# One pass for both blocks of local attention, paired cross scores, one first transfer and another landing time

## The chip, the cores and the metric

The kernel runs on one core of a Trainium2 chip. The metric is the device time of one execution in microseconds. The core's engines run side by side, each with its own queue in order: TensorE (PE) multiplies matrices, VectorE (DVE) and ScalarE (ACT) work on elements, GpSimd (POOL) and SyncE (SP) issue transfers (DMA) from and to memory. An engine that needs another's result waits on a semaphore.

## The reference

One step of a decoder layer for a prompt of 256 tokens and 8 sequences of 8 new tokens each (320 columns together), width 2048, in fp32. Cut to what matters:

```python
z = rmsnorm(x, g_mix) @ w_in            # B, C, h, local q/k/v, cross q
y_conv = b * short_conv(c * h)
y_swa  = sink_attention(q, k, v, bias, valid, sink)   # 8 heads, 2 kv heads, window 128
mk, mv = memory_kv(mem_prompt)          # 256 memory tokens
y_x    = cross_attention(qx, mk, mv)    # 4 heads
x = x + concat(y_conv, y_swa, y_x) @ w_out
x = x + square(relu(rmsnorm(x, g_mlp) @ w_up)) @ w_down
```

Local attention of the prompt goes by blocks of 128 queries. A block sees itself and the block before, with a band mask of 128 positions and a relative-position bias; each head has a learned sink in the softmax's denominator. So the first block has 128 keys and the second 256, of which any query sees at most 128: key j of the block before is seen by a query i only if i < j, and key j of the own block only if i >= j. A new token of a sequence sees 128 cached keys and those of its own 8 tokens. Cross attention of the sequences reads 256 cached memory tokens each.

## The kernel before

All activations lie with channels in the partitions and the 320 tokens in the free dimension. fp32 accuracy comes from splitting: a weight or activation is divided into a high part (ACT rounds it) and a low part (DVE subtracts), and PE multiplies high by high, high by low, low by high: three main matmuls for a product. Weights come in pieces of 512 KB (128 partitions, 2 x 512 columns) into `raw`; `split_piece` makes `wh` and `wl`. Four pieces may be loaded and four split ahead of PE.

The program is written out by one Python pass. The main work is a list of units, each 12 main matmuls of the projections (6 wider ones for the memory's weights): cross queries, local keys and values, memory keys and values, local queries, C, h, B, then output, up and down projections. Between units, `boundary` lets side jobs take a step: the norm of x (`rb_job`, `mean_rsqrt`), the heads' norms (`start_head`), the memory (`mem_job`), cross attention of prompt and sequences (`cross_prompt`, `cross_sample`), local attention (`swa_prompt`, `swa_sample`), the convolution. What a job issues in a step stands between two units in every engine's queue: on PE a burst of small matmuls, named "ax" by the PSUM tile that they write; the main ones are "mm".

Where a job steps is set by `Pace`, a running estimate of each engine's clock made while the program is written. A job that needs a tile yields in `after` until the estimate says that the tile was ready 0.2 us ago on PE's clock. A load counts as landed LAG us after its estimated transfer (2 us for weights). These estimates only set the order; at run time semaphores keep it right, and a burst that was set too early makes PE wait.

What the prediction's steps touch: `rb_job` squares the four blocks of x (tiles `lx`) on ACT and adds them up on DVE. `mean_rsqrt` then takes the mean over the partitions with `mean_over`: ACT makes the high part of the sum, DVE the low part, PE multiplies both by a matrix of 1/2048 (`mean_d`). From this comes rb, with which every projection's result is scaled. `start_head` does the same for each head, with `mean_h`. At the start, `cols` (all gain columns, 252 bytes for each partition) and the first 320 columns of x come by ACT's queue; 10 matmuls on a tile of ones run on PE ahead of the first main one. `cross_sample` computes four sequences at a time: scores of one sequence are four matmuls, one for each head, in 32-column tiles of the array; its values are eight. `swa_prompt` does two heads, one block after the other. `swa_sample` does four sequences for one kv head. The tiles that side jobs use are `w2` (12 of 512 columns), `z` (10 of 336) and four PSUM banks.

The profile names nearly every instruction by line 166, the helper in `Paced` through which all of them are issued.

Of the kernel before, what the change touches and what calls it, by code (L numbers as in the profile page):

```python
# [34 lines left out]
LAG = 6.0  # L35
WARM = 10
# [9 lines left out]
def arrange(inputs):  # L46
# [15 lines left out]
    out["cols"] = np.concatenate([a[n].reshape(-1, P) for n, _ in ROWS]).T  # L62
# [5 lines left out]
def constants():  # L68
# [11 lines left out]
    for r in row:  # L80
# [4 lines left out]
        "c_ident": np.eye(P, dtype=np.float32),  # L85
        "c_hot": hot,
# [161 lines left out]
def trunk_step(ctx: ExitStack, tc: tile.TileContext, I, O):  # L248
# [29 lines left out]

    def zt(cols=336):
        return zs.need([P, 336])  # L280
# [14 lines left out]
    act.dma_start(out=cols[:, 0:63], in_=I["cols"])  # L295
# [9 lines left out]
    dve.memset(ones_h, 1.0 / 128)  # L305
    ones_d = const.tile([P, P], F32, name="ones_d")
    dve.memset(ones_d, 1.0 / D)
    mean_h = const.tile([P, P], F32R, name="mean_h")
    dve.tensor_copy(out=mean_h, in_=ones_h)
    mean_d = const.tile([P, P], F32R, name="mean_d")  # L310
    dve.tensor_copy(out=mean_d, in_=ones_d)
# [12 lines left out]
    def gcol(name, i=0):  # L324
        return cols[:, col[name] + i:col[name] + i + 1]
# [82 lines left out]
    def split_piece():  # L408
# [9 lines left out]
        if i < 2:  # L418

            for c in range(2):  # L420
                k = 2 * i + c
                x = xblk[0][:, k, :]
                if k:
                    split_act(S0h[:, k, :], S0l[:, k, :], x, gcol("g_mix", k))
                else:
                    dve.tensor_scalar(out=S0h[:, k, :], in0=x, scalar1=gcol("g_mix", k), scalar2=None, op0=ALU.mult)
                    dve.scalar_tensor_tensor(out=S0l[:, k, :], in0=x, scalar=gcol("g_mix", k),
                                             in1=S0h[:, k, :].bitcast(F32), op0=ALU.mult, op1=ALU.subtract)
# [149 lines left out]
    def rb_job():  # L578
        for b in range(4):
            act.activation(out=xblk[b], in_=xblk[b], func=AF.Square)  # L580
# [155 lines left out]
    def mk_evac(t, ps):  # L736
        z = w2.must([P, 512])
# [118 lines left out]
    def cross_sample(f):  # L856
# [15 lines left out]
        for _ in range(2):  # L872
            yield from load()
        sb = yield from bank()
        for b in range(4):
            cur = queue.pop(0)
            yield from after(*cur)
# [5 lines left out]
            yield from load()  # L883
# [50 lines left out]
    def sink_softmax(s, nh, sinks, nsinks):  # L934
        nm, es, den = sm()[:, 0:nh], sm()[:, 0:nh], sm()[:, 0:nh]
        dve.tensor_reduce(out=nm, in_=s, axis=AX.X, op=ALU.max, negate=True)
        dve.tensor_tensor(out=nm, in0=nm, in1=nsinks, op=ALU.min)
        dve.tensor_tensor(out=es, in0=sinks, in1=nm, op=ALU.add)
        yield from after(es)
        for i in range(nh):  # L940
# [5 lines left out]
        for i in range(nh):  # L946
            dve.tensor_scalar(out=s[:, i, :], in0=s[:, i, :], scalar1=den[:, i:i + 1], scalar2=None, op0=ALU.mult)

    def swa_prompt(g, hp):
# [7 lines left out]
        for blk in range(2):  # L957
            nkb = 1 + blk
            nk = nkb * P
            q0 = blk * P  # L960
            bk = yield from bank()
            for i in range(2):
                pe.matmul(out=bk[:, i * nk:(i + 1) * nk], lhsT=qT[:, hs + i, q0:q0 + P], rhs=kT[:, g, 0:nk],
                          start=True, stop=True)
            yield 1
            s = yield from half()
            s3 = s[:, 0:2 * nk].rearrange("p (h k) -> p h k", h=2)
            dve.scalar_tensor_tensor(out=s3, in0=bk[:, 0:2 * nk].rearrange("p (h k) -> p h k", h=2), scalar=SC,
                                     in1=b3[:, :, 256 - nk:256], op0=ALU.mult, op1=ALU.add)
            ax.put(bk)  # L970
            yield from sink_softmax(s3, 2, skb[:, hs:hs + 2], nskb[:, hs:hs + 2])
            yield from after(s)
            bk = yield from bank()
            for kb in range(nkb):
                for i in range(2):
                    c = (kb * 2 + i) * P
                    pe.transpose(bk[:, c:c + P], s3[:, i, kb * P:(kb + 1) * P], ident)
            yield 1
            pt = yield from half()
            act.activation(out=pt[:, 0:2 * nk], in_=bk[:, 0:2 * nk], func=AF.Copy)  # L980
            ax.put(bk)
# [420 lines left out]
```

## Time and profile before

| | us |
|---|---|
| median of 3 runs | 1315.78 |
| lowest, highest | 1315.7, 1315.86 |
| the profiled execution's own time | 1315.88 |
| its span, first to last instruction | 1313.8 |
| busy: PE, DVE, ACT, POOL | 1309.0, 675.2, 540.3, 18.4 |
| mean granted TensorE clock | 1.0 |

The span is counted from the first instruction; 2.1 us lie around it. In the profile a group reads "out<-in": the tile written and the tiles read, buffer numbers left out. A row of the timeline gives start, duration, engine, line and operation, and in brackets the idle time ahead of it with what ended it. A PE matmul's record covers its pipeline too, so records overlap and what counts is the distance from start to start. An fp32 matmul stands there as two records, a transpose or an fp32r matmul as one.

### The profile page before, as it was taken

Reading aid. Unit: us, or ns where it says so; the run is one execution under the profiler, and the core shown is the slowest. Engines: PE = TensorE matmul, PEld = TensorE weight load, DVE = VectorE, ACT = ScalarE, POOL = GpSimd, SP = SyncE. Lnnn points to the kernel's source line nnn. Section 1 sums busy time; section 2 is a strip of 40 time slices with the busy share of each in tenths; the row PEclk is TensorE's granted clock in tenths of the full one; section 3 lists DMA queues with packets and bytes.
Section 4 is the critical chain, followed back from the end, with each engine's and each line's share of the span. In section 5 each row is a group of like instructions: output and inputs, shape, how many; then the busy total and the mean of one; then the engine's idle time right before and its main releaser. Section 6 shows DMA issues by size and latency. Waiting matters only on the chain.

```text
span 1313.8 us, 21565 instructions
## 1 busy us (share of the span) xinstructions
PE 1309.0 (100%) x8956; PEld 1287.4 (98%) x8956; DVE 675.2 (51%) x1025; ACT 540.3 (41%) x801; POOL 18.4 (1%) x37
## 2 busy tenths in 40 slices
PE   9999999999999999999999999999999999999998
PEld 9988999999999999999999999999999999999998
DVE  7876665776576445443345443345443344444342
ACT  7683554343355444322344422334432324433321
POOL 1011000000000000000000000000000000000000
PEclk9999999999999999999999999999999999999999
DMA  8767555356344443444443444443444444444552
GB/s 298 254 208 273 180 173 198 132 190 249 129 159 148 156 147 128 161 158 149 156 148 129 161 158 149 154 150 128 161 159 148 155 149 129 160 157 150 176 167 73
DMA packets 65488, 217.03 MB, mean 165 GB/s; under 512 B 8437, under 2 KB 10717, under 8 KB 65360
## 3 DMA queue, kind: packets, MB, share of 16 engines
q1 hardware_dynamic: 63184, 210.14, 47.9%
q0 software_dynamic: 1776, 5.26, 1.2%
q8 instruction: 70, 1.15, 0.4%
q10 hardware_dynamic: 432, 0.28, 0.1%
q14 instruction: 26, 0.21, 0.0%
HBM read 211.53 MB, written 7.65 MB: 167 GB/s over the span
## 4 chain that ended last, share of the span: by engine, by line
PE 96%; DMA 1%; ACT 1%; DVE 1%; issue 1%; ACTq 0%; DVEq 0%; SPq 0%
PE mm L166 92%; PE ax L166 3%; DMA raw<-in_w_in 1%; DMA lx<-in_xT 1%; ACT wh L166 0%; DVE wl L166 0%; DVE lx L166 0%; ACT lx L166 0%; DVE S1l L166 0%; DVE S0l L166 0%; ACT w L166 0%; ACT S1h L166 0%; ACT S0h L166 0%; DVE z L166 0%; ACTq L166 0%
## 5 line engine op out<-in xcount | busy, mean ns | idle before, releaser
L166 DVE TENSOR_TENSOR wl<-raw,wh 128x1024 fp32r<-128x1024 f32 (+1 forms) x362 | 436.1, 1217 | 476.5 <-ACT wh L166 475.4
L166 ACT ACTIVATE wh<-raw 128x1024 fp32r<-128x1024 f32 (+1 forms) x362 | 374.4, 1050 | 631.6 <-PE mm L166 595.6
L166 PE MATMUL mm<-S0h,wh 128*128 128x320 f32 x1472 | 456.2, 311 | 0.0
L166 PE MATMUL mm<-S0h,wl 128*128 128x320 f32 x1472 | 453.0, 309 | 0.0
L166 PE MATMUL mm<-S0l,wh 128*128 128x320 f32 x1472 | 452.8, 309 | 0.0
L166 PE MATMUL mm<-S1h,wh 128*128 128x320 f32 x1280 | 397.3, 310 | 0.4 <-DVE lx L166 0.4
L166 PE MATMUL mm<-S1h,wl 128*128 128x320 f32 x1280 | 395.5, 309 | 0.0
L166 PE MATMUL mm<-S1l,wh 128*128 128x320 f32 x1280 | 395.5, 309 | 0.0
L166 PEld LDWEIGHTS mm<-S0h,wh 128*128 128x128 f32 x1472 | 276.3, 188 | 2.8 <-issue 2.7
L166 PEld LDWEIGHTS mm<-S0l,wh 128*128 128x128 f32 x1472 | 276.0, 188 | 0.1
L166 PEld LDWEIGHTS mm<-S0h,wl 128*128 128x128 f32 x1472 | 275.9, 188 | 0.1
L166 PEld LDWEIGHTS mm<-S1h,wh 128*128 128x128 f32 x1280 | 240.3, 188 | 1.1 <-ACT wh L166 0.6
L166 PEld LDWEIGHTS mm<-S1l,wh 128*128 128x128 f32 x1280 | 240.4, 188 | 0.1
L166 PEld LDWEIGHTS mm<-S1h,wl 128*128 128x128 f32 x1280 | 240.3, 188 | 0.0
L166 DVE TENSOR_TENSOR lx<-mm,lx 128x320 f32<-128x320 f32 (+1 forms) x97 | 46.9, 486 | 80.6 <-PE mm L166 75.3
L166 ACT ACTIVATE z<-z 128x320 f32<-128x320 f32 (+1 forms) x118 | 55.1, 470 | 65.3 <-DVE z L166 64.2
L166 DVE TENSOR_TENSOR S1l<-z,S1h 128x320 fp32r<-128x320 f32 x68 | 33.3, 490 | 51.1 <-ACT S1h L166 51.1
L166 ACT ACTIVATE S1h<-z 128x320 fp32r<-128x320 f32 x68 | 32.1, 472 | 9.0 <-DVE z L166 6.9
L166 DVE SCALAR_TENSOR_TENSOR z<-mm,r2b 128x320 f32<-128x320 f32 x64 | 31.0, 484 | 0.0
L166 PE MATMUL mm<-wh,S1h 128*128 128x512 f32 x64 | 25.7, 401 | 0.0
L166 PE MATMUL mm<-wh,S1l 128*128 128x512 f32 x64 | 25.1, 392 | 0.0
L166 PE MATMUL mm<-wl,S1h 128*128 128x512 f32 x64 | 25.0, 390 | 0.0
(162 smaller groups left out, 433.1 us busy)
## 6 DMA issues: line engine op xcount, KB each, us to landing
raw<-in_w_up SPq DMA_DIRECT2D x128, 512.0 KB, 3.3
raw<-in_w_down SPq DMA_DIRECT2D x128, 512.0 KB, 3.3
raw<-in_w_in SPq DMA_DIRECT2D x54, 512.0 KB, 4.0
raw<-in_w_out SPq DMA_DIRECT2D x32, 512.0 KB, 3.5
raw<-in_w_mem_k SPq DMA_DIRECT2D x8, 512.0 KB, 4.7
raw<-in_w_mem_v SPq DMA_DIRECT2D x8, 512.0 KB, 3.9
w<-in_cmk SPq DMA_DIRECT2D x16, 256.0 KB, 5.2
w<-in_cmv SPq DMA_DIRECT2D x16, 256.0 KB, 4.6
```

Of the source, the lines that this page charges most:

```text
L166: return f(*args, **kw)
```

## The change

It has six parts.

1. **Local attention of the prompt in one pass.** Both blocks of two heads are scored together into two PSUM banks (`banks`). For the second block the scores against the block before (`prev`) and against its own keys are laid over each other with a maximum: at each place just one of the two is not masked. So a row of the softmax has 128 places for either block, and one softmax serves four rows of heads. The transposed weights are divided again by a triangle of ones (`tri`, a new constant that POOL loads): `low` is the part for the own block, and the rest belongs to the block before. The value product is one matmul over all four for the first block's values and one more, over 256 columns, for the second's.
2. **Local attention of the sequences**: `swa_sample` now does all eight for a kv head in one job.
3. **Cross scores**: `cross_sample` waits for two sequences' keys and issues their matmuls in one step; the loads follow by twos.
4. **The start**: the gain columns and the first block of x come in one transfer, into a `w2` tile named `first`; DVE copies the columns out. The first four channel blocks take their gain straight from `first`. In `rb_job` the first block's square is two instructions, since its parts lie in two tiles. The table load on ACT now stands ahead of the transfer. WARM is 8 for 10, and one tile serves for both mean matrices.
5. **The clock**: LAG is 5.5 for 6.0. With it, and with the other jobs, every decision of `Pace` may fall elsewhere.
6. `mk_evac` runs the side jobs until the memory job is done, if it isn't.

```diff
-LAG = 6.0
-WARM = 10
+LAG = 5.5
+WARM = 8
...
+    def banks():
+
+        while sum(last is None or pace.idle(last) for _, last in ax.free) < 2:
+            yield 1
+        return ax.must([P, 512]), ax.must([P, 512])
...
-    act.dma_start(out=cols[:, 0:63], in_=I["cols"])
...
     def rb_job():
         for b in range(4):
-            act.activation(out=xblk[b], in_=xblk[b], func=AF.Square)
+            if b:
+                act.activation(out=xblk[b], in_=xblk[b], func=AF.Square)
+            else:
+                act.activation(out=xblk[0][:, 0, :], in_=first[:, 63:63 + T], func=AF.Square)
+                act.activation(out=xblk[0][:, 1:4, :], in_=xblk[0][:, 1:4, :], func=AF.Square)
+                w2.put(first)
...
     def mk_evac(t, ps):
+        side.until(["mem"])
...
         for _ in range(2):
             yield from load()
+        yield from after(*queue[0], *queue[1])
         sb = yield from bank()
         for b in range(4):
             cur = queue.pop(0)
-            yield from after(*cur)
+            yield from after(*cur, *(queue[0] if b % 2 == 0 else ()))
...
             w2.put(*cur)
-            yield from load()
+            if b % 2:
+                yield from load()
+                yield from load()
...
+        bk, fk = yield from banks()
+        for i in range(2):
+            pe.matmul(out=bk[:, i * 256:(i + 1) * 256], lhsT=qT[:, hs + i, P:TP], rhs=kT[:, g, 0:TP],
+                      start=True, stop=True)
+            pe.matmul(out=fk[:, i * P:(i + 1) * P], lhsT=qT[:, hs + i, 0:P], rhs=kT[:, g, 0:P], start=True, stop=True)
...
+        dve.tensor_tensor(out=s[:, 256:512], in0=s[:, 256:512], in1=prev[:, 0:256], op=ALU.max)
...
+        for r in range(4):
+            pe.transpose(bk[:, r * P:(r + 1) * P], s4[:, r, :], ident)
+        yield 1
+        pt = yield from half()
+        low = yield from zt()
+        dve.tensor_tensor(out=pair(low[:, 0:256]), in0=pair(bk[:, 256:512]),
+                          in1=tri.rearrange("p (o k) -> p o k", o=1).to_broadcast([P, 2, P]), op=ALU.mult)
+        act.activation(out=pt, in_=bk, func=AF.Copy)
+        dve.tensor_tensor(out=pt[:, 256:512], in0=pt[:, 256:512], in1=low[:, 0:256], op=ALU.subtract)
...
+        pe.matmul(out=bk, lhsT=vnat[:, 0, g * P:(g + 1) * P], rhs=pt, start=True, stop=False, skip_group_check=True)
+        pe.matmul(out=bk[:, 256:512], lhsT=vnat[:, 1, g * P:(g + 1) * P], rhs=low[:, 0:256], start=False, stop=True,
+                  skip_group_check=True)
...
+    def swa_sample(g):
...
+        pool.dma_start(out=tri, in_=I["c_tri"])
...
-    load_x(0, 0, 1, act)
+
+    first = w2.must([P, 512])
+    act.dma_start(out=first[:, 0:63 + T], in_=I["cols"])
```

How the instructions stand, before and after, at the three places that the prediction speaks of. Numbers in the names count the tiles made.

PE where the mean over x is taken: the pair on `mean_d` between main matmuls of the local key and value group. mm_524 is that group's first output tile in both programs; the second is mm_548 before and mm_546 now, the third mm_565 before. Before:

```order
L166 MATMUL mm_548<-S0h_116,wh_420 128x320
L166 MATMUL mm_548<-S0l_117,wh_420 128x320
L166 MATMUL mm_548<-S0h_116,wl_421 128x320
L166 MATMUL ax_3_498<-z_2_499,mean_d_104 128x320
L166 MATMUL ax_3_498<-z_3_500,mean_d_104 128x320
L166 MATMUL mm_565<-S0h_116,wh_388 128x320
```

Now:

```order
L167 MATMUL mm_524<-S0h_115,wh_421 128x320
L167 MATMUL mm_524<-S0l_116,wh_421 128x320
L167 MATMUL mm_524<-S0h_115,wl_422 128x320
L167 MATMUL ax_3_497<-z_2_498,mean_d_99 128x320
L167 MATMUL ax_3_497<-z_3_499,mean_d_99 128x320
L167 MATMUL mm_546<-S0h_115,wh_389 128x320
```

The pair stands behind the first tile's 12 matmuls instead of the second's: main matmuls 0 to 203 are ahead of it instead of 0 to 215. The first burst on `mean_h` moves likewise, from 348 main matmuls to 324, and holds two heads instead of one.

DVE ahead of that pair: the additions of squares (lx), the low parts of the memory's blocks (S1l), four small ones on the sinks, and the low part of the sum (z_3). Before:

```order
L166 TENSOR_TENSOR wl_421<-raw_275,wh_420 128x1024
L166 SCALAR_TENSOR_TENSOR S1l_119<-w2_1_315,cols_92,S1h_118 128x256
L166 TENSOR_TENSOR lx_1_127<-lx_1_127,lx_3_145 128x1280
L166 TENSOR_TENSOR lx_1_127<-lx_1_127 128x640
L166 TENSOR_TENSOR lx_1_127<-lx_1_127 128x320
L166 SCALAR_TENSOR_TENSOR S1l_119<-w2_1_315,cols_92,S1h_118 128x256
L166 TENSOR_TENSOR sm_468<-skb_109,sel_110 128x8
L166 TENSOR_REDUCE skc_111<-sm_468 128x2
L166 TENSOR_SCALAR nskc_113<-skc_111 128x2
L166 TENSOR_SCALAR nskb_112<-skb_109 128x8
L166 SCALAR_TENSOR_TENSOR S1l_119<-w2_2_317,cols_92,S1h_118 128x256 x2
L166 TENSOR_TENSOR z_3_500<-lx_1_127,z_2_499 128x320
```

Now:

```order
L167 TENSOR_TENSOR wl_422<-raw_274,wh_421 128x1024
L167 TENSOR_TENSOR lx_1_131<-lx_1_131,lx_3_145 128x1280
L167 TENSOR_TENSOR lx_1_131<-lx_1_131 128x640
L167 TENSOR_TENSOR lx_1_131<-lx_1_131 128x320
L167 SCALAR_TENSOR_TENSOR S1l_118<-w2_2_314,cols_92,S1h_117 128x256
L167 TENSOR_TENSOR sm_467<-skb_108,sel_109 128x8
L167 TENSOR_REDUCE skc_110<-sm_467 128x2
L167 TENSOR_SCALAR nskc_112<-skc_110 128x2
L167 TENSOR_SCALAR nskb_111<-skb_108 128x8
L167 SCALAR_TENSOR_TENSOR S1l_118<-w2_2_314,cols_92,S1h_117 128x256
L167 SCALAR_TENSOR_TENSOR S1l_118<-w2_3_316,cols_92,S1h_117 128x256
L167 TENSOR_TENSOR z_3_499<-lx_1_131,z_2_498 128x320
```

One S1l ahead of the additions is gone, and a memory block's two halves now lie one behind the additions and one behind the small ones. On ACT the square of that block (it waits for the second half), one S1h and then the high part z_2 follow each other, without the two copies and the S1h that stood between before. Further on in DVE's queue, rb and the first heads' scaling by it stand one weight split sooner than before.

PE at the first cross scores (a row with x2 is two matmuls, so four records). Before:

```order
L166 MATMUL ax_13_1116<-w2_18_1108,w2_5_444 32x256 x2
L166 MATMUL ax_13_1116<-w2_19_1110,w2_5_444 32x256 x2
L166 MATMUL mm_1147<-wh_1123,S1h_118 128x512
L166 MATMUL mm_1147<-wl_1124,S1h_118 128x512
L166 MATMUL mm_1147<-wh_1123,S1l_119 128x512
L166 MATMUL mm_1151<-wh_1123,S1h_118 128x512
L166 MATMUL mm_1151<-wl_1124,S1h_118 128x512
L166 MATMUL mm_1151<-wh_1123,S1l_119 128x512
L166 MATMUL ax_14_1227<-z_32_1099,w2_17_1096 128x272
L166 MATMUL ax_13_1116<-w2_20_1112,w2_5_444 32x256 x2
L166 MATMUL ax_13_1116<-w2_21_1114,w2_5_444 32x256 x2
```

Now:

```order
L167 MATMUL ax_13_1209<-w2_19_1105,w2_6_443 32x256 x2
L167 MATMUL ax_13_1209<-w2_20_1107,w2_6_443 32x256 x2
L167 MATMUL ax_13_1209<-w2_21_1109,w2_6_443 32x256 x2
L167 MATMUL ax_13_1209<-w2_22_1111,w2_6_443 32x256 x2
L167 MATMUL mm_1146<-wh_1119,S1h_117 128x512
```

Two sequences' scores stand in one burst. So it is at all four places. Of the values' four bursts, each of two sequences before, two remain so and two are now divided into bursts of one sequence, with main matmuls between.

More of the change, by code (lines that the diff above doesn't have):

```diff
@@ L956, in swa_prompt @@
         yield from after(bias, qT, kT)
[L957 to L981, printed above, removed]
-            w2.put(s)
-            yield from after(pt, vnat)
-            bk = yield from bank()
-            for kb in range(nkb):
-                pe.matmul(out=bk[:, 0:256], lhsT=vnat[:, kb, g * P:(g + 1) * P], rhs=pt[:, kb * 256:(kb + 1) * 256],
-                          start=kb == 0, stop=kb == nkb - 1)
-            yield 1
-            w2.put(pt)
-            yield from put_mix(lambda m: m[:, 4 + hs:6 + hs, q0:q0 + P], bk[:, 0:256].rearrange("p (h q) -> p h q", h=2))
-            ax.put(bk)
@@ L998, in load @@
             return t
-        kt = yield from load(I["csk"])
-        vc = yield from load(I["csv"])
-        yield from after(kt, qs, kT)
-        bk = yield from bank()
-        q4 = qs[:, g, bg * 4:bg * 4 + 4].rearrange("p b h t -> p (b h t)")
-        for b in range(4):
-            pe.matmul(out=bk[b * 32:(b + 1) * 32, 0:P], lhsT=q4[:, b * 32:(b + 1) * 32],
-                      rhs=kt[:, b * P:(b + 1) * P], start=True, stop=True, tile_position=(0, b * 32))
-        pe.matmul(out=bk[:, P:192], lhsT=q4, rhs=kT[:, g, TP:T], start=True, stop=True)
@@ L1009, in swa_sample @@
-        yield 1
-        w2.put(kt)
-        s = yield from zt()
-        for lo, hi, o in ((0, P, 0), (P, 192, bg * 64)):
-            dve.scalar_tensor_tensor(out=s[:, lo:hi], in0=bk[:, lo:hi], scalar=SC,
-                                     in1=st["bsx"][:, g * 256 + o + lo:g * 256 + o + hi], op0=ALU.mult, op1=ALU.add)
+        kt, vc = [], []
+        for l, n in ((kt, "csk"), (vc, "csv")):
+            for bg in range(2):
+                t = yield from load(I[n], bg)
+                l.append(t)
@@ new lines, in swa_sample @@
+        yield from after(*kt, qs, kT)
+        bk = yield from bank()
+        for bg in range(2):
+            c = bg * 192
+            q4 = qs[:, g, bg * 4:bg * 4 + 4].rearrange("p b h t -> p (b h t)")
+            for b in range(4):
+                pe.matmul(out=bk[b * 32:(b + 1) * 32, c:c + P], lhsT=q4[:, b * 32:(b + 1) * 32],
+                          rhs=kt[bg][:, b * P:(b + 1) * P], start=True, stop=True, tile_position=(0, b * 32))
+            pe.matmul(out=bk[:, c + P:c + 192], lhsT=q4, rhs=kT[:, g, TP:T], start=True, stop=True)
@@ L1329, in trunk_step @@
     ax.put(bk)
+    dve.tensor_copy(out=cols[:, 0:63], in_=first[:, 0:63])
     dve.tensor_scalar(out=cols[:, 63:66], in0=cols[:, 60:63], scalar1=-0.5, scalar2=None, op0=ALU.mult)
```

129 lines of the change are left out of this document (84 added, 45 removed).

## The prediction

> **What bounds the kernel now.** The page first: engines, then the chain of work that ended last.
>
> ```profile
> span 1313.8 us, 21565 instructions
> PE 1309.0 (100%) x8956; PEld 1287.4 (98%) x8956; DVE 675.2 (51%) x1025; ACT 540.3 (41%) x801; POOL 18.4 (1%) x37
> PE mm L166 92%; PE ax L166 3%; DMA raw<-in_w_in 1%; DMA lx<-in_xT 1%; ACT wh L166 0%; DVE wl L166 0%; DVE lx L166 0%; ACT lx L166 0%; DVE S1l L166 0%; DVE S0l L166 0%; ACT w L166 0%; ACT S1h L166 0%; ACT S0h L166 0%; DVE z L166 0%; ACTq L166 0%
> ```
>
> TensorE is never free. "mm" are the projections, which the change leaves alone; "ax" are the small matmuls of attention and norms, 3% of the span, set between them. Any gain must come out of that 3% or out of PE's waits, so I read those next: the waits of PE and of its weight loads.
>
> ```profile
> PE ax L1328 <- DVE ones L166: 1.1, 1, 1.1
> PE mm L166 <- DVE lx L166: 0.4, 1, 0.4
> PEld mm L166 <- ACT wh L166: 1.0, 2, 0.6
> PEld ax L166 <- DVE z L166: 0.7, 2, 0.4
> ```
>
> Columns: total us, times, longest. The first is the start of the warm-up and stays. No side load (cached keys, values, bias) appears, so PE never waits for one. The last row is the one that matters below: side matmuls on z.
>
> Next, the chain in order of time, where PE's work can be priced: start, us, what, how many.
>
> ```profile
> 64.89 1.39 PE mm L166 x6
> 97.39 0.57 PE ax L166 x8
> 97.96 1.59 PE mm L166 x6
> 139.01 1.01 PE ax L166 x32
> 140.02 1.95 PE mm L166 x12
> 281.44 0.44 PE ax L166 x4
> 281.88 1.76 PE mm L166 x12
> 416.48 894.09 PE mm L166 x6096
> ```
>
> A main matmul costs 894.09/6096 = 0.147 us, and 12 of them 1.76. The x8 row is one sequence's cross scores (four matmuls in column tiles, two records each): 0.57 for itself, and the six main matmuls behind it take 1.59 instead of 1.39, so 0.77 in all. The x32 row is two sequences' values: 1.01 and 1.95 - 1.76 = 0.19, so 1.20. A group of eight records has 256 columns in the scores and 128 in the values. With w for eight records at 128 columns and o for going into column tiles and out again, o + 2w = 0.77 and o + 4w = 1.20: w = 0.215, **o = 0.34 us for each burst**. Transposes pay nothing of the kind: four take 0.44, and the 12 main matmuls behind take the plain 1.76; 0.11 each.
>
> **The change, part by part.** First what PE no longer does, from the changed order.
>
> Cross scores: eight bursts of x8 become four of x16. Four times o goes: -1.36 us. The new pacing also cuts two of the four x32 value bursts into two x16 each, two o more: +0.68. Local prompt attention: 24 transposes become 16, 8 x 0.11 = -0.88. Its scores stay two matmuls of 256 and two of 128 columns per job, and its value product one of 512 and one of 256 for three of 256: equal columns. fp32 at 512 columns stands in no row; I take it by columns. Local sample attention: equal matmuls, with the value bursts going from three to two; 0 to 0.34 less, I take 0.2, since the scores there change mode as often as before. Sum on PE: -1.36 + 0.68 - 0.88 - 0.2 = **-1.76 us**. The softmax merging, copies and evictions saved on DVE and ACT are worth nothing directly: those engines are half idle and PE covers them. Were that cover gone, the smaller work would help, not hurt.
>
> Next the pacing: with another landing time the order of the bursts moves. Places with PE slack of microseconds lose nothing by it. One place has none. Here are PE, DVE and ACT (timeline rows: start, us, engine, what) around the sum of squares of x, whose mean gives rb:
>
> ```profile
> 38.57 0.31 PE L166 MATMUL mm<-S0h,wl 128*128 128x320 f32 x1
> 38.72 0.84 PE L166 MATMUL ax<-z,mean_d 128*128 128x320 f32 x2
> 39.39 0.31 PE L166 MATMUL mm<-S0h,wh 128*128 128x320 f32 x1
> 31.22 1.22 DVE L166 TENSOR_TENSOR wl<-raw,wh 128x1024 fp32r<-128x1024 f32 x1
> 32.36 0.48 DVE L166 SCALAR_TENSOR_TENSOR S1l<-w,cols,S1h 128x256 fp32r<-128x256 f32 x1
> 32.75 1.48 DVE L166 TENSOR_TENSOR lx<-lx,lx 128x1280 f32<-128x1280 f32 x1
> 34.27 1.35 DVE L166 TENSOR_TENSOR lx<-lx 128x640 f32<-128x640 f32 x2
> 35.54 0.48 DVE L166 SCALAR_TENSOR_TENSOR S1l<-w,cols,S1h 128x256 fp32r<-128x256 f32 x1
> 35.94 0.16 DVE L166 TENSOR_TENSOR sm<-skb,sel 128x8 f32<-128x8 f32 x1
> 36.41 0.16 DVE L166 TENSOR_SCALAR nskb<-skb 128x8 f32<-128x8 f32 x1
> 38.60 0.48 DVE L166 TENSOR_TENSOR z<-lx,z 128x320 fp32r<-128x320 f32 x1
> 36.05 0.63 ACT L166 ACTIVATE w<-w 128x512 f32<-128x512 f32 x1 [3.89 <-DVE S1l L166]
> 36.59 0.49 ACT L166 ACTIVATE S1h<-w,cols 128x256 fp32r<-128x256 f32 x1
> 36.99 0.42 ACT L166 ACTIVATE w<-mm 128x320 f32<-128x320 f32 x1
> 23.13 1.26 ACT L166 ACTIVATE lx<-lx 128x1280 f32<-128x1280 f32 x1
> ```
>
> The mean is two matmuls, on the high part of the sum (from ACT) and on its low part (DVE, 38.60 to 39.08). A pair takes about 0.30 when nothing waits (2 x 0.147); here it is 39.39 - 38.72 = 0.67, so PE waited 0.37 us. In the changed order the pair stands 12 main matmuls earlier: PE would be there at 38.72 - 1.76 = 36.96. Is z earlier too? I put the new order of DVE and ACT on these rows. DVE: wl at 31.22, +0.1 because the first block's square is now two instructions on a full ACT (bounds 0 and 0.2: a whole one is 1.26, and 320 columns elsewhere 0.42). Then the additions at 32.46 with no S1l ahead (S1l to next: 0.39), 33.98 for the next two, S1l at 35.25, the four small ones 35.65 to 36.28 (they took 35.94 to 36.57), the next S1l to 36.76. ACT's square of the memory block waits for that: 36.79, then S1h at 37.33 (0.54 later, as before), done 37.82, and the high part runs 37.73 to 38.18. DVE's S1l starts when S1h is done, 37.85, and the low part 0.40 behind it: 38.25 to 38.73. PE's second matmul starts 0.06 later as now, main matmuls again at 39.03. Without a wait they would run at 36.96 + 0.30 = 37.26: PE waits 1.77 us, 0.37 before. **+1.40 us.** Bounds: 0, if the pair's inputs come 1.8 us earlier than I make it, and 1.8.
>
> Now the start: one transfer for two, warm-up 8 for 10, the table load ahead of the transfer in ACT's queue.
>
> ```profile
> 0.74 0.41 ACTq L166 DMA_DIRECT2D cols<-in_cols  x1
> 1.22 0.42 ACTq L166 DMA_DIRECT2D lx<-in_xT  x1
> 4.92 0.39 DVE L166 TENSOR_SCALAR S0h<-lx,cols 128x320 fp32r<-128x320 f32 x1 [0.58 <-DMA lx<-in_xT]
> 5.45 1.29 PE L166 MATMUL mm<-S0h,wh 128*128 128x320 f32 x4
> 6.58 0.75 PE L166 MATMUL mm<-S0l,wh 128*128 128x320 f32 x4
> 10.97 1.06 ACT L166 ACTIVATE wh<-raw 128x1024 fp32r<-128x1024 f32 x1 [0.23 <-DMA raw<-in_w_in]
> 12.06 1.23 DVE L166 TENSOR_TENSOR wl<-raw,wh 128x1024 fp32r<-128x1024 f32 x1 [0.73 <-ACT wh L166]
> 13.34 0.41 PE L166 MATMUL mm<-S0h,wl 128*128 128x320 f32 x1
> ```
>
> The block of x was asked for at 1.22 and released DVE at 4.92; asked for some 0.4 us sooner, less about 0.2 us for copying the columns, it may start PE 0.2 to 0.4 us earlier, and the shorter warm-up (10 matmuls filled PE to 5.45) lets it. But the third weight piece arrives by its own transfer: 10.97 on ACT, 12.06 to 13.29 on DVE, and PE stood there already at 13.34 (the row lasts 0.41 where its neighbours last 0.31). What PE gains ahead of that it waits there. And whatever is left, up to 1.8 us of gain or of loss, goes into the wait at 37 us, which ends with DVE and ACT whatever PE did. So I put **0** for the start, and 0 for eight warm-up matmuls even if they should leave the clock low for longer; bounds -0.2 and +0.2, by which the ACT-DVE chain itself may shift with the landing of the weights (the 64 KB of the triangle go through the same engines).
>
> The other landing time also lets side matmuls go up to 0.5 us nearer to their loads. No load is among the waits, so 0; the upper bound is a wait of 0.4, as on z. The wait for the reloaded x behind the first output group (0.4, on lx) keeps its place: 0.
>
> **Sum**, against the profiled execution: 1315.88 (span 1313.8 and 2.1 around it) - 1.76 + 1.40 = 1315.52, 0.36 less. The median of the runs is 1315.78, so about **1315.4 us**. A measurement tells about 0.2%, 2.6 us, from no change.
>
> **Rivals.**
> (B) *The pair does not wait longer.* Then the PE savings stand alone: 1315.78 - 1.76 = 1314.0. For it: DVE and ACT are half idle on average. Against: in these rows they run back to back until 32 us, and each later step waits for the other engine.
> (C) *The same again at the heads*, slower than before. The mean for the first two heads moves 24 main matmuls earlier, to 324 from 348. If its chain (rb, scaling, square, split) kept its distance from the mean, 58.75 - 39.39 = 19.4 us, it would be ready at 39.03 + 19.4 = 58.4, while PE is there after 120 matmuls, at 39.03 + 17.6 = 56.7: 1.7 us more, 1317.1. It decides from the point where that chain is more than 17.6 us behind the mean. For it: this row of before shows a pair of 0.41 (58.75 to 59.16), already 0.1 late. Against: DVE's new order has rb and the heads' scaling by it one weight split sooner.
>
> ```profile
> 58.75 0.57 PE L166 MATMUL ax<-z,mean_h 128*128 128x320 f32 x2
> 59.16 0.31 PE L166 MATMUL mm<-S0h,wh 128*128 128x320 f32 x1
> ```
>
> (D) *The clock falls in the longer wait.* At the start PE takes 6.58 - 5.45 = 1.13 us for four matmuls, twice the later 0.59, and is at full rate only 5.5 us after its first instruction at 1.1 (the first row of the waits). If a wait of 1.8 us brought that back for 5.5 us, half of it would be lost: +2.7, 1318.1. Against: the wait is broken by the first matmul of the pair, and no wait of before was followed by such a rate. [...]
> (E) *No effect at all*, since the bursts only move: 1315.8. It lies within the forecast.
>
> **How the numbers follow.** Forecast 0.62 with E, B 0.17, C 0.12, D 0.04, others 0.05. The range reaches from B less the start's 0.2 and the sample bursts' further 0.14 to C plus 0.3 for pieces not seen: 1313.6 to 1317.4; D and others stay out. By over 0.2% faster would be under 1313.15: B with further gains, 0.06. Slower, over 1318.4: D or C with more, 0.06. The rest, 0.88, lies within.
>
> **What would show it.** Right: no cross score burst of x8, only x16; no pair of transposes for a first block; the pair on mean_d near 37 to 39 us taking, with the gap ahead of it, about 2 us; first main matmul near 5.1 with a longer wait near 13. Wrong: a mean_d pair of 0.3 us (B), a mean_h burst over 0.8 us (C), main matmuls of 0.28 us after 39 (D), or a new row in PE's waits that names a load.

## The result and the profile after

| | before | changed |
|---|---|---|
| median of the runs, us | 1315.82 (4 runs) | 1322.48 (4 runs, 1321.91 to 1324.87) |
| profiled execution, us (span) | 1315.88 (1313.8) | 1322.86 (1320.8) |
| ratio of the medians | | 1.0054, 95% interval 1.0041 to 1.0068 |

The changed kernel is 6.7 us slower, 0.54%. The prediction was 1315.4 with a range up to 1317.4: wrong, and on the wrong side.

The page of the changed kernel: its span and its engines.

```profile
span 1320.8 us, 21479 instructions
PE 1310.4 (99%) x8936; PEld 1286.7 (97%) x8936; DVE 673.3 (51%) x998; ACT 537.6 (41%) x784; POOL 18.6 (1%) x38
```

DVE and ACT have 2 to 3 us less to do each, as the merging promised, and PE has 20 instructions fewer. Yet the span is 7.0 us longer while PE is busy only 1.4 us longer: it stands still. Who it waits for, in the view of PE's waits (total us, times, longest):

```profile
PE mm L167 <- DVE lx L167: 3.0, 1, 3.0
PE ax L167 <- ACT z L167: 1.4, 1, 1.4
PE ax L1379 <- DVE ones L167: 1.1, 1, 1.1
PE ax L167 <- DMA w<-in_cmk: 0.9, 2, 0.5
```

Before, the row on lx was 0.4, and there was no row on a load. The prediction named such a row as what would show it wrong. (A wait of the weight load ahead of a matmul stands in another view, so 0.9 is not all that the cached keys cost; 2.9 stand there.) I go through the four places in order of time.

**The mean over D**, on PE's timeline:

```profile
36.44 0.31 PE L167 MATMUL mm<-S0h,wl 128*128 128x320 f32 x1
38.18 0.98 PE L167 MATMUL ax<-z,mean_d 128*128 128x320 f32 x2 [1.44 <-ACT z L167]
39.00 0.31 PE L167 MATMUL mm<-S0h,wh 128*128 128x320 f32 x1
```

Main matmuls go on at 39.00; the prediction had worked out 39.03. Before, they went on at 39.39, but 12 main matmuls (1.76 us) further: 39.00 against 37.63 is a loss of 1.37 us, 1.40 foreseen. The 0.37 us that the new start gained ahead of this place (PE there at 36.44, before it would have been at 36.81) went into the wait, as foreseen too.

**The cached keys of the second two sequences**, on the same view:

```profile
109.88 0.39 PE L167 MATMUL mm<-wh,S1l 128*128 128x512 f32 x1
110.62 1.99 PE L167 MATMUL ax<-w,w 128*32 128x256 f32 x12 [0.36 <-DMA w<-in_cmk]
113.16 0.63 PE L167 MATMUL ax<-w,w 128*32 128x256 f32 x4 [0.55 <-DMA w<-in_cmk]
113.71 0.50 PE L167 MATMUL mm<-wh,S1h 128*128 128x512 f32 x1
```

One burst of 16 is torn into 12 and 4, and from main matmul to main matmul it takes 113.71 - 109.88 = 3.83 us. Where the keys are there in time (the run e12 below) the same burst takes 1.32: **2.5 us of wait**. SyncE's queue shows when their loads were asked for, in the timeline of the changed kernel:

```profile
100.79 4.09 SPq L167 DMA_DIRECT2D raw<-in_w_in  x3
104.97 1.81 SPq L167 DMA_DIRECT2D w<-in_cmk  x4
```

and of the kernel before, with PE's first burst on these keys:

```profile
96.74 3.83 SPq L166 DMA_DIRECT2D raw<-in_w_in  x3
100.67 2.76 SPq L166 DMA_DIRECT2D w<-in_cmk  x4
109.09 0.64 PE L166 MATMUL ax<-w,w 128*32 128x256 f32 x8
```

Three weight loads stand ahead of them in both kernels, and these wait for weight splits to give their buffers back. The first of the three goes out at 100.79 instead of 96.74, since the split that it waits for (wl on DVE) runs at 99.54 instead of 95.49, and that split's half on ACT at 98.47 instead of 94.42. ACT was until then at the heads' norms and at exponentials, and the weight piece itself landed at 98.42; which of the two held the split up, this trace doesn't tell. So the keys are asked for 4.3 us later (the last at 106.4, before at 102.1). They take as long as before to land, 5.6 to 6.7 us (5.4 to 6.0): the last is there at 113.1, before at 108.1. Before, PE used them in bursts at 109.09 and 111.25, some 3 us behind their landing; now it is there at 110.1, with all four loads still to land.

**The reloaded x**, in the chain of waits from 300 us (start, us, what):

```profile
301.20 0.10 ACT sm L167
301.29 0.96 ACT wh L167
...
302.28 1.24 DVE wl L167
...
303.53 0.33 SPq L167
...
303.91 4.76 DMA lx<-in_xT
...
308.76 0.50 DVE lx L167
...
309.40 5.29 PE mm L167 x24
```

Read it upwards: PE waits for a PSUM bank, which DVE frees by adding the output group to x, which lands at 308.67; its load was asked for at 303.91, behind a weight load (the SPq row of 0.33) that had to wait until a weight split (wl on DVE) gave its buffer back; that split waited for its half on ACT (wh), and ACT was at the exponentials of the local softmax (sm) until 301.29. PE had come to the place at 306.26 (its last main matmul starts at 306.11): 3.14 us of wait, 0.51 before. The load of x and PE behind the wait, in the kernel before:

```profile
296.25 1.94 SPq L166 DMA_DIRECT2D lx<-in_xT  x4
301.86 0.38 PE L166 MATMUL mm<-S1h,wh 128*128 128x320 f32 x1 [0.35 <-DVE lx L166]
```

**The clock behind it**: the view of windows (the last columns are PE's granted clock, the DMA share and GB/s):

```profile
310.00:313.40 3.40, 3.40 (x15) 3.40 (x14) 3.33 (x11) 0.00 (x0) 0.00 (x0) 0.52 1.01 394
313.40:316.00 2.60, 2.60 (x20) 2.60 (x20) 2.53 (x8) 0.00 (x0) 0.00 (x0) 0.97 0.70 249
```

Half the clock for 3.4 us: the main matmuls stand 0.267 us apart there, 0.147 elsewhere. From 310.07 to 313.65 there are 14 of them: 3.58 us for 2.06, a loss of **1.5 us**. The page's row of 40 slices and the mean clock of 0.999 hide it.

The sum against the profiled execution of before: 1.37 (mean) + 2.5 (keys) + 2.63 (x, 3.14 - 0.51) + 1.5 (clock) + some 0.6 in small waits on local keys and softmax rows = 8.6; the difference is 6.98. So PE's own work is about **1.6 us** shorter (1.76 foreseen). That is a remainder and carries the errors of the other terms. One part of it can be read directly: a whole burst of 16 cross scores (98.54 us, with what the main matmul behind it takes longer) costs 1.21 us, and two bursts of 8 before cost 2 x 0.77 = 1.54: 0.33 us less for each merged pair, 0.34 foreseen.

### The profile page after: what moved, and what is told of

It is laid out like the page before. It is cut to its first block, busy times and chain, and to the rows that moved or that the text cites. A ratio compares the mean times of both kernels' runs of the same rounds, so it can differ in the third digit from the quotient of the medians.

```text
span 1320.8 us, 21479 instructions
## 1 busy us (share of the span) xinstructions
PE 1310.4 (99%) x8936; PEld 1286.7 (97%) x8936; DVE 673.3 (51%) x998; ACT 537.6 (41%) x784; POOL 18.6 (1%) x38
## 4 chain that ended last, share of the span: by engine, by line
PE 96%; DVE 1%; DMA 1%; issue 0%; SPq 0%; ACT 0%; DVEq 0%; ACTq 0%
PE mm L167 93%; PE ax L167 3%; DVE wl L167 1%; DMA w<-in_cmk 1%; DMA raw<-in_w_mem_v 0%; DMA lx<-in_xT 0%; SPq L167 0%; PE ax L1379 0%; DVE lx L167 0%; ACT wh L167 0%; DVE z L167 0%; DVE S1l L167 0%; ACT w L167 0%; ACT S1h L167 0%; DVE w L167 0%
```

## The experiments

In all of them the time is the median, and the ratio is to the kernel before on the same chip. The kernel before took 1315.82 to 1315.92 us in every round, so medians are compared across rounds too.

### Is it the landing time?

e1: the changed kernel with the old landing time.

```diff
-LAG = 5.5
+LAG = 6.0
```

> The changed kernel with the landing time put back from 5.5 to 6.0; everything else as changed. In its order the mean_d pair stays 12 main matmuls earlier than before, and the second burst of 16 cross scores still follows the first by 42 main matmuls. Theory S (the loss comes from the structure of the change: pairs of cached keys loaded only after a whole burst, wider softmaxes ahead of a weight split): the wait on mean_d stays near 1.7 us, the waits on cached keys at the second burst stay near 2 us, and the time stays at 1319 to 1322.5 us. Theory K (the loss comes from the landing time, side work set 0.5 us nearer to its loads): no row of PE's waits names cached keys any more, the wait on the reloaded x falls below 1 us, no main matmul at half rate behind it; 1314 to 1316 us.

1323.63 us, ratio 1.0058 (1.0043 to 1.0073). Its waits of PE:

```profile
PE mm L167 <- DVE lx L167: 2.8, 1, 2.8
PE ax L167 <- DVE z L167: 1.5, 2, 1.2
PE ax L167 <- ACT z L167: 1.2, 1, 1.2
PE ax L167 <- DVE w L167: 1.2, 1, 1.2
```

A miss for both. The constant does not make the loss: without it the kernel is as slow. But the waits on cached keys are gone, against theory S, and others (z, w) have come.

e2: the kernel before with the new landing time alone.

```diff
-LAG = 6.0
+LAG = 5.5
```

> The kernel before with nothing but the landing time 5.5 instead of 6.0. Its mean_d pair stays where it was, so about 0.4 us of wait there under both theories; three of its four value bursts of 32 records become two of 16, some 1 us more. Theory K (the landing time causes the loss): new rows for cached keys or for the reloaded x among PE's waits, and 1318 us or more. Theory S (the structure does): no such rows, 1315.8 to 1317 us.

1323.91 us, ratio 1.0062 (1.0047 to 1.0077): this constant alone costs 8.1 us, but at another place. PE's timeline:

```profile
281.86 0.60 PE L166 MATMUL ax<-ident,w 128*128 128x128 f32 x4
286.50 0.65 PE L166 MATMUL ax<-w,qs 128*32 128x128 f32 x8 [4.04 <-DMA w<-in_csk]
```

The cached local keys took 10.3 us to land there. The clock is at 0.50 from 285.6 us, inside the wait, to 292.4, so for 5.9 us behind it (worked out from the mean clocks of three windows: 0.89 from 282 to 286.6 us, 0.50 from 287.5 to 290.8, 0.80 from 290 to 296). By the letter this is theory K's outcome; but with e1, where the old constant leaves the changed kernel as slow, either theory was too simple: a shift of half a microsecond in the model lays the side work anew, and it is a matter of the order that comes out whether, and where, a late input is hit.

### The cached keys

e3: the scores again one sequence at a time.

```diff
-        yield from after(*queue[0], *queue[1])
...
-            yield from after(*cur, *(queue[0] if b % 2 == 0 else ()))
+            yield from after(*cur)
...
-            if b % 2:
-                yield from load()
-                yield from load()
+            yield from load()
```

> The changed kernel with the cross scores again one sequence at a time (four bursts of 8 records for two of 16 in each half, loads one pair after each); all else as changed. My theory: the waits of PE and of its weight loads on cached keys (together about 2.3 us in the changed kernel) go, and the bursts cost 1.36 us more, so some 0.9 us less in that stretch. The rest of the order moves too: if the reloaded x at the first output group still comes 3 us late, with the half rate behind it, the time is 1321 to 1322; if that wait goes, 1316 to 1318. Rival: the cached keys' waits are the transfers' own delay and stay with single loads too; 1323 to 1324.

1326.57 us, ratio 1.0079 (1.0064 to 1.0094), worse than every case I had written down.

```profile
PE ax L167 <- DMA w<-in_cmk: 2.6, 2, 2.0
PE ax L167 <- DMA w<-in_csk: 1.9, 1, 1.9
```

Single loads do not cure it. With the landing time of 5.5 the third sequence's burst was set only 24 main matmuls behind the second's, and its keys, asked for behind two weight loads, were again late. The pairing by itself is not the cause. The clock, too, fell in this execution: it is 0.52 from 39.6 to 43 us, behind a wait of 1.77 us, and behind one of 1.97 us main matmuls of 512 columns stand 0.43 us apart (113.39 to 114.25 us) that stood 0.23 apart ahead of it. The mean clock is 0.996, so some 5.3 of 1325 us are lost: by estimate three stretches of 3.4 us at half rate, the third perhaps behind the 1.9 us on the cached local keys.

e12: the changed kernel with the second burst of the first half three steps later.

```diff
             yield from after(*cur, *(queue[0] if b % 2 == 0 else ()))
+            if b == 2 and f == 0:
+                yield 3
```

> The changed kernel with the second burst of 16 cross scores of the first half put 18 main matmuls (2.6 us) later; the loads of its cached keys stay where they are. Theory: PE's 2.3 us of waits there come from keys that land 0.6 to 3.2 us after PE gets to the burst; 2.6 us later none or at most 0.6 us is left: 1.7 to 2.3 us less, 1320 to 1321 us, with the waits on x and mean_d as in the changed kernel. Rival: the loads move along with PE, the wait stays, 1322 to 1323 us.

1321.1 us, ratio 1.0037 (1.0024 to 1.005): 1.4 us less than the changed kernel, for the 1.7 to 2.3 expected (the single runs, 1320.05 to 1322.53, overlap with the changed kernel's), and no row on these keys is left. The burst is whole:

```profile
114.10 0.39 PE L167 MATMUL mm<-wh,S1l 128*128 128x512 f32 x1
114.42 1.07 PE L167 MATMUL ax<-w,w 128*32 128x256 f32 x16
115.42 0.42 PE L167 MATMUL mm<-S0h,wh 128*128 128x320 f32 x1
```

The loads stayed where they were, PE came later, and the wait went: the burst had been set too early by the model. The waits on x (2.7) and on the mean (1.0) stayed.

### The reloaded x

e4: its loads in GpSimd's queue instead of SyncE's.

```diff
-        sp.dma_start(out=t, in_=I["xT"][:, 4 * g:4 * g + 4, :])
+        pool.dma_start(out=t, in_=I["xT"][:, 4 * g:4 * g + 4, :])
```

> The changed kernel with the four reloads of x issued from GpSimd's queue instead of SyncE's, where they stand behind a weight load that waits for a weight split. The order of all other instructions is unchanged. My theory (the reload was late because of what stood ahead of it in its queue): the wait of 3.0 us on the reloaded x is gone, and with it the stretch of main matmuls at half rate behind it (1.7 us): 4 to 5 us less, 1317.5 to 1318.7. Rival (the four tiles were not free earlier, or the transfer itself was slow): the wait stays above 2 us, 1321 to 1323. Rival (the half rate has another cause than the wait): the wait goes and the half rate stays, 1319 to 1320.

1327.88 us, ratio 1.0093 (1.0072 to 1.0114). The wait on x went, as expected, but the time rose by 5.4 us: GpSimd waits for nothing there and asked for 2.6 MB at 277.6 us, ahead of the copies of the old cache and of the cached local keys. The view of DMA issues from 276 to 285 us (KB each, median us to landing):

```profile
lx<-in_xT POOLq DMA_DIRECT2D x4, 640.0 KB, 9.0
...
out_old_k<-in_cache_swa_k POOLq DMA_DIRECT2D x1, 960.0 KB, 16.5
...
w<-in_csk SPq DMA_DIRECT2D x2, 256.0 KB, 13.3
```

The keys took 13.3 us, and PE waited 6.3 us for them. One late input was exchanged for another.

e5: the copies of the old cache moved out of that stretch.

```diff
-            pool.dma_start(out=O[f"old_{n}"].rearrange("b t g d -> b (t g d)"),
-                           in_=I[f"cache_swa_{n}"][0, :, 8:128].rearrange("b t g d -> b (t g d)"))
...
+            add_group(I["w_up"], c * 2048 + g * 512, order, xa, up_evac(g),
+                      pre={1: lambda: old("k"), 3: lambda: old("v")} if c == 0 and g == 1 else None)
```

(`old` issues the same copy on SyncE.)

> The changed kernel with the two copies of the old local cache into the outputs (960 KB each, issued by GpSimd near 278 us) moved into the second group of w_up, issued by SyncE between weight loads there. All other instructions keep their order. Theory Q (those copies fill the DMA engines just when weight loads, the bias and the cached local keys are fetched, and so make the weight split, the weight load behind it and the reloaded x late): weight loads issued at 280 to 283 us land 3 us or more earlier, the wait on the reloaded x falls under 1 us, no half rate follows, 1318 us. Theory V (the reloaded x is late because DVE and ACT have a backlog of softmax work ahead of the weight splits near 288 to 302 us, whatever the copies do): the wait on x stays near 3 us with the half rate behind it, 1321.5 to 1323 us.

1323.05 us, ratio 1.0056 (1.0039 to 1.0072); the wait on x is 3.0 as it was. Theory Q fell: the copies do not make x late.

e11: but do they make the keys late that e2 waited for? The kernel before with the landing time 5.5 and the same move of the copies.

```diff
-LAG = 6.0
+LAG = 5.5
...
-            pool.dma_start(out=O[f"old_{n}"].rearrange("b t g d -> b (t g d)"),
...
+                      pre={1: lambda: old("k"), 3: lambda: old("v")} if c == 0 and g == 1 else None)
```

> The kernel before with the landing time 5.5 and the copies of the old cache moved from near 275 us into w_up. With the landing time alone PE waited 4.3 us at 282 us for the cached local keys, with main matmuls at half rate behind that. If the copies held those keys up (their load was asked for at 276 us, behind 1.9 MB of copies), the wait falls under 1 us and the half rate goes: 1316 to 1317.5 us. If the keys are only asked for too late: the wait stays at 3 to 4 us, 1322 to 1324 us.

1317.22 us, ratio 1.0009 (0.9999 to 1.0019), 6.7 us under e2, with no row on a load among PE's waits. In the same view the keys now take:

```profile
w<-in_csk SPq DMA_DIRECT2D x1, 256.0 KB, 5.0
```

5.0 us for 10.3. So the copies are what e2 met, and not what made x late in the changed kernel.

e6: the loads of x two weight loads earlier in SyncE's queue.

```diff
-                  needs={0: ["cp", "cs0", "cs1"], 1: ["conv", "convout"]} if g == 0 else None,
-                  pre={1: lambda: pre_out(0, 1, 2, 3)} if g == 0 else None)
+                  needs={0: ["cp", "cs0", "cs1", "convout"], 1: ["conv"]} if g == 0 else None,
+                  pre={0: lambda: pre_out(0, 1, 2, 3)} if g == 0 else None)
```

> The changed kernel with the four reloads of x put two weight loads earlier in SyncE's queue; all other instructions keep their order. My theory (x was late because its load stood behind a weight load that waited for a weight split): the load is issued near 298 instead of 304 us and lands near 304, before PE needs it at 306; the wait of 3.0 us and the half rate behind it (1.7 us) are gone, 1317.5 to 1318.5 us. Rival (the 2.6 MB ahead of two weight loads makes those late in their turn): a new wait on a weight split of 1 to 4 us behind 306 us, 1319 to 1323 us.

1319.92 us, ratio 1.003 (1.0018 to 1.0042). SyncE's queue and a window behind:

```profile
300.14 1.93 SPq L167 DMA_DIRECT2D lx<-in_xT  x4
```

```profile
310.00:313.40 3.40, 3.40 (x27) 3.40 (x26) 3.12 (x10) 1.06 (x1) 0.00 (x0) 1.00 1.04 424
```

Asked for at 300.1 instead of 303.9, x is there in time; no wait on it, no late split behind it, the full clock. The gain is 2.6 us and not the 4 to 5 expected. The profiled execution lost the clock at another place, the wait for the mean over D (below); of the six executions the three with a mean clock of 1.000 took 1317.25 to 1319.27 us, the three with 0.999 took 1320.57 to 1321.86.

e13: what held up the weight load ahead of x? One of the two merged local softmaxes of the second key head is taken out of the stretch.

```diff
         yield from after(bias, qT, kT)
+        if g == 1 and hp == 1:
+            yield 12
```

> The changed kernel with the second of the two local prompt jobs of the second key head held back 12 steps: its scores move from 1500 to 1644 main matmuls, behind the place at 1632 where PE waits for the reloaded x; so only one merged softmax (of 4 x 128 rows by keys) stands on DVE and ACT ahead of the weight splits near 295 to 302 us. Queues and loads keep their order there. Theory V (the backlog of two merged softmaxes at once delays the splits, these the weight load in SyncE's queue, and that the load of x): the wait on x falls from 3.0 us to under 1.5 us and no half rate follows, 1318 to 1320 us. Rival W (the splits wait for something else, such as weight pieces that land late or PE's release of the split buffers): the wait stays at 2.5 to 3.3 us, 1321.5 to 1323 us.

1318.5 us, ratio 1.0023 (1.0013 to 1.0033; single runs 1317.45 to 1322.79), 4.0 us under the changed kernel. The chain again:

```profile
295.04 1.54 ACT w L167 x8
296.58 0.10 ACT sm L167
...
297.70 1.07 ACT wh L167
...
298.79 1.23 DVE wl L167
...
300.05 0.33 SPq L167
...
300.42 4.83 DMA lx<-in_xT
```

One softmax (four exponentials, w x8 with the reads of their sums) ahead of the split instead of two: the split on ACT runs at 297.70 for 301.29, x is asked for at 300.42 for 303.91, and the wait falls from 3.0 to 0.3. Theory V stands.

### The clock

e7: eight matmuls on ones, whose result nothing reads, inside the wait on x.

```diff
+        if u == 0 and un["base"] == out_base[0]:
+            bk = ax.must([P, 512])
+            for _ in range(8):
+                nc.tensor.matmul(out=bk[:, 0:P], lhsT=ones, rhs=ones, start=True, stop=True)
+            ax.put(bk)
```

> The changed kernel with eight matmuls on ones (nothing reads their result) put on PE at the head of the second w_out group, into the wait for the reloaded x; they leave the wait's end where it is. They take 8 x 0.22 = 1.8 us of the idle time, so that PE stands still for some 1.3 us instead of 3.1. If the half rate behind the wait comes from PE standing still for that long: no main matmul of 0.267 us behind it, 1.7 us less, 1320.5 to 1321 us. If it comes from something else there (the full DMA engines, the reload): the half rate stays, 1322 to 1323 us.

1321.73 us, ratio 1.0046 (1.0031 to 1.0061). PE's timeline, and the window:

```profile
306.25 0.31 PE L167 MATMUL mm<-S1h,wl 128*128 128x320 f32 x1
306.40 1.95 PE L495 MATMUL ax<-ones 128*128 128x128 f32 x16
309.20 0.38 PE L167 MATMUL mm<-S1h,wh 128*128 128x320 f32 x1 [0.85 <-DVE lx L167]
```

```profile
310.00:313.40 3.40, 3.40 (x27) 3.39 (x26) 3.33 (x11) 0.00 (x0) 0.00 (x0) 1.00 1.01 402
```

Nothing useful was added and x came no sooner (309.20 against 309.40), the DMA engines are as full as without (1.01), and yet the clock stays at 1.00. The mean clock of all four executions is 1.000 here, and 0.997 to 1.000 in the changed kernel. So the half rate here is made by PE standing still: the idle time in the bracket is 0.85 us, and 2.98 in the changed kernel. In the profile it is gone entirely; the median gained only 0.8 us of the 1.5, between the two cases written down, and how much of that is the spread of the other waits I can't tell.

### All together

e9: the changed kernel with the landing time 7.5 alone.

```diff
-LAG = 5.5
+LAG = 7.5
```

> The changed kernel with nothing but the landing time 7.5 instead of 5.5. The mean_d pair stays 12 main matmuls early, so its wait of 1.2 to 1.9 us stays. If the waits on cached keys come from modelled landings shorter than the measured 5.6 to 6.7 us, they go (2.3 us). The side work around 300 us is laid anew; with local scores moved behind the first output group, the backlog of DVE and ACT ahead of the weight splits is smaller, and x may come in time: then 1315 to 1316.5 us. If x stays late, with the half rate: 1318 to 1320 us.

1317.9 us, ratio 1.0017 (1.0008 to 1.0026; single runs 1316.97 to 1320.45). No wait on cached keys and none on x: with this order the local scores of the second key head come behind the first output group. The time lies 1.4 us above what was expected for that case. Left are the mean over D (1.5) and 1.5 on other means.

e8: three edits more: the mean over D one step later, x two weight loads earlier, and the copies in w_up (the last two as above).

```diff
-LAG = 5.5
+LAG = 7.5
...
         yield from after(sq)
+        yield 1
         bk = yield from bank()
         yield from mean_over(bk, sq, mean_d)
```

> The changed kernel with four edits: landing time 7.5, the mean over D one step later, the reloads of x two weight loads earlier, the copies of the old cache moved into w_up. If the losses are the waits named so far and nothing else, all go: the mean_d pair stands two dozen main matmuls later and waits 0 to 0.4 us, no wait on cached keys or on x, no half rate; 1313.5 to 1315 us, under the kernel before. Rival (each change of the landing time or of a step lays the side work anew, and lands some of it on other late inputs): new waits of 1 to 5 us at other places, 1316 to 1321 us.

1313.74 us, ratio 0.9983 (0.9974 to 0.9993). What PE waits for besides the start of the warm-up:

```profile
PE ax L167 <- DVE z L167: 0.7, 1, 0.7
PE mm L167 <- DVE S0h L167: 0.4, 1, 0.4
```

e14: the same without the move of the copies.

```diff
-LAG = 5.5
+LAG = 7.5
...
         yield from after(sq)
+        yield 1
...
-                  pre={1: lambda: pre_out(0, 1, 2, 3)} if g == 0 else None)
+                  pre={0: lambda: pre_out(0, 1, 2, 3)} if g == 0 else None)
```

> The kernel of 1313.7 us with the copies of the old cache left where the changed kernel has them, near 278 us. With the landing time 7.5 the cached local keys are asked for well ahead of PE there, so if the copies matter only where a load has little room: 1313.5 to 1314.5 us. If the copies hold up the keys or the weight pieces in this order too: a wait on cached local keys or a weight split of 1 to 4 us, 1315 to 1319 us.

1313.33 us, ratio 0.9982 (0.9973 to 0.9991): the copies need not move where no load has little room. This is the **fastest version**, 2.5 us under the kernel before and 9.2 under the changed one.

e10: the kernel before with the four edits of e8, and the change's line in `mk_evac`.

```diff
-LAG = 6.0
+LAG = 7.5
...
     def mk_evac(t, ps):
+        side.until(["mem"])
...
         yield from after(sq)
+        yield 1
...
+                  pre={0: lambda: pre_out(0, 1, 2, 3)} if g == 0 else None)
...
+                      pre={1: lambda: old("k"), 3: lambda: old("v")} if c == 0 and g == 1 else None)
```

> The kernel before with the four edits of the run at 1313.7 us (landing time 7.5, the mean over D one step later, the reloads of x two weight loads earlier, the copies of the old cache in w_up) and the one line of the change that makes the memory keys wait for their norm. So it lacks only the merged bursts, merged softmaxes and the new start. If PE's savings are worth what the prediction put on them (1.8 us), it takes 1315 to 1316 us; if the merging is worth nothing on PE and the four edits made all of the gain, 1313.5 to 1314 us.

1318.05 us, ratio 1.0015 (1.0006 to 1.0025). That is above both cases written down. The edits by themselves do not make the kernel before faster; with the rest of the change (merged attention, paired scores, the new start) they do. The 4.3 us between e8 and e10 are more than PE's 1.8: the order that comes out is again another one, with 1.4 us more in waits of PE, the old start lacks the 0.37 us, and some 0.8 us stay open. So e10 doesn't price the merging by itself. It shows that the change as a whole is worth something in an order without late inputs, and the changed kernel lost it by its order.

## Why the prediction was wrong

- **PE's savings, -1.76: right in size, as far as it can be read.** What is left over in the sum above is -1.6, and a merged burst of scores saves 0.33.
- **The mean over D, +1.40: right**, +1.37. Other executions with the same order there had PE idle for 0.9 to 1.8 us in the bracket ahead of the pair, so the size varies by about half a microsecond from run to run.
- **The start, 0: right.** PE came 0.37 us sooner to the mean and waited that long there. The longer wait near 13 us, named as a sign, did not come: PE is past that place at 13.00 for 13.34, so the third weight piece was sooner too.
- **Rival C did not come**: the first burst on `mean_h`, two heads at 56.60 us, takes 0.58 us to the next main matmul, four times 0.147.
- **The landing time, "No load is among the waits, so 0; the upper bound is a wait of 0.4": the step that failed first.** It read the slack of the order before and applied it to an order that the change had rebuilt; so did "Places with PE slack of microseconds lose nothing by it". The keys had landed some 3 us ahead of their use; the change asks for them 4.3 us later and uses them at about the same time. 2.5 us. The landing times in the profile (5.4 to 6.0 us on these keys, beside a model of 5.5 that takes no account of what a load ahead in the queue waits for) would have shown that the model was now too short. The constant alone is not the fault: with 6.0 (e1) the keys are in time, and other late inputs make the changed kernel as slow.
- **The reloaded x, "keeps its place: 0": the second.** The place was kept, and the time was not: what stood ahead of the load in SyncE's queue came 2.7 us later relative to PE (x was asked for at 296.25 before and at 303.91 now, 7.66 later; PE's last main matmul ahead of the place starts at 301.19 and at 306.11, 4.92 later). That the work saved on DVE and ACT is "worth nothing directly: those engines are half idle and PE covers them" was the deeper fault. Half idle is a mean; the merged softmaxes do less work in all but more at once, and e13 shows that two of them in one stretch hold up the weight split, and so the load. 2.6 us.
- **Rival D, the half clock: right as a mechanism, wrong as to the place and the size.** The 0.04 that I gave it at the wait of the mean was an estimate; the trace of before has no such wait. It came at a wait that I had not seen, for 3.4 us and not 5.5, and cost 1.5 us. It can come at the mean too: e6 and e3 had it there (clock 0.51 and 0.52 from 39.6 to 43 us), behind idle times of 1.41 and 1.77 us; the changed kernel's 1.44 us had none behind it (1.00).
- **The range** held nothing of these, because each unknown was bounded by the waits of before. A change that lets a model lay out all side work anew needs the price of a new late input in its range; here one such place cost from 2.5 us (the keys) to about 7 us (e2: 4.3 of wait and 2.7 by the clock behind it).

## What to carry over

Where a static model decides the order, compare what the new order asks for with the measured landing times and with the queue ahead of each load, place by place; the waits of the old order say nothing of it. Two engines that are half idle on average (DVE 51% busy, ACT 41%) can still be late by microseconds in the stretch where the work was merged (the split on ACT at 301.29 us behind two merged softmaxes, at 297.70 behind one). When a late input is found, look for the cause of the instruction that stands ahead of its load in the queue, and leave the model some room (here 7.5 us for loads that took 5 to 6.7): the same merged kernel was 0.54% slower or 0.18% faster than before by that and two small moves.

## What was not expected of the hardware

PE's clock fell behind some short waits. It is low behind 2.98 us in the changed kernel (0.52 from 310 to 313.4 us), 2.8 in e1 (0.72 from 308 to 314), 4.0 in e2 and 6.3 in e4 (below). Ahead of the pair on the mean the waits of 0.93 to 1.31 us (e5, e4, e12, e7, e1 and e13) have a clock of 1.00 behind them, from 39.6 to 43 us. In between it went both ways: 1.41 us in e6 and 1.77 and 1.97 in e3 had the half rate behind them, 1.44 in the changed kernel and 1.54 in e9 had not. For the 3.0 us in e5 and the 2.7 in e12 there is only the mean clock of the execution, 0.998 in both. The idle time in the bracket ahead of the pair on the mean is 1.41 us in e6, and the window behind it has a clock of 0.50:

```profile
39.70:43.00 3.30, 3.30 (x14) 3.30 (x14) 3.26 (x5) 3.25 (x7) 1.10 (x1) 0.50 0.29 87
```

It is 1.54 us in e9, and the same window has 1.00:

```profile
39.70:43.00 3.30, 3.30 (x25) 3.30 (x24) 3.25 (x5) 3.22 (x7) 1.03 (x1) 1.00 0.36 107
```

So one such wait cost about 1.5 us more behind it: 1.5 behind the 2.98 us of the changed kernel, and 1.6 behind the 1.41 of e6 (11 matmuls of 0.147 us fewer than e9 in the same window). Behind the waits of 1.41 us in e6, 1.77 in e3, 2.8 in e1 and 2.98 in the changed kernel the mean clocks of the windows come to 3.4 us at 0.50 each time (reckoned with 1.00 for the rest). The longest waits cost more: in e2 (4.0 us) and e4 (6.3 us) the clock fell before the wait had ended and stayed at 0.50 for 5.9 and 5.4 us behind it (e2 as above; in e4 0.93 from 290 to 296 us and 0.51 from 296 to 302, so low from 295.2 to 301.9).

The length of the wait does not decide alone: 1.41 us in e6 had the half clock behind it, 1.54 in e9 had not. What else decides was not shown.

The other thing is the price of a bulk copy: 1.9 MB from DRAM to DRAM made 256 KB of keys land in 10.3 us instead of 5.0 (e2 and e11), and with 2.6 MB of x in front of it 13.3 (e4).
